# Which gate products run beside the attention heads, and which in their tail: an encoder layer in fp32 on one core

## The chip, the core and the metric

The kernel runs on one core of a Trainium2 chip. Its engines work side by side, each through its own list of instructions in order: TensorE (PE in the profile) multiplies, VectorE (DVE) and ScalarE (ACT) work on elements, GpSimd (POOL) works on elements in SBUF, SyncE (SP) issues most transfers, and ScalarE issues some. SBUF is the working memory, PSUM receives the products in banks, DRAM holds inputs, outputs and spilled intermediate results. The metric is the device time of one execution in microseconds, as the median of several runs; shorter is better.

## The reference

One layer of an encoder, on x of 1024 tokens by 1024 channels in float32:

```
h = rmsnorm(x, g_mix)
z = h @ w_in                      # 512 pooling channels | q | k | v
y_pool = pool_mixer(u_pool)       # windows 2, 4, 8, 16; mean - self; a 128x128 map per group; scale
y_attn = diff_attention(q, k, v)  # 8 heads, two softmax maps each, ALiBi, causal by chunks of 64
gates = sigmoid(h @ w_gate + b_gate)          # 1024 x 2048
merged = gates[:, :1024] * (y_pool @ w_branch_pool) + gates[:, 1024:] * (y_attn @ w_branch_attn)
x = x + merged @ w_out
x = x + square(relu(rmsnorm(x, g_ffn) @ w_up)) @ w_down
```

The change concerns the time in which `gates` (before the sigmoid) and `y_pool @ w_branch_pool` are computed.

## The kernel before, in words

**Products.** Every product of two matrices is made of three matmuls (`mm3`, lines 122 to 124): each operand is split into a high part, rounded to the type that TensorE takes, and a low part, the rest; high times high, high times low and low times high are summed in PSUM. `split` (lines 116 and 117) makes the parts: a cast on ScalarE, then a subtraction on VectorE, or on GpSimd for most weights.

**Heads.** h is normalised and transposed into h^T, which stays in SBUF as parts of high and low for both halves of the tokens. Then eight heads of eight token blocks each go through a pipeline of stages: A makes z (24 matmuls of 384 columns), B normalises q and k, C transposes them, D makes scores and the softmax, E transposes the result, F multiplies by v, H and R norm. The order in a step is written in `O`. The result of a head goes to DRAM (`y_dram`).

**Filler.** The code after the heads traces work that doesn't depend on them, and a scheduler that works through a model of the machine sets it between the heads' instructions: an instruction that comes earlier in the program has the higher priority, and a tile is had when its room (one of a pool's fixed number of buffers) is free. So the list of each engine is fixed at build time. The fillers are

- `pool_group(g)`, the pooling mixer of one of four groups: 48 matmuls, sums on VectorE, then a small product; to `p_dram`.
- `gate_cols(c)`, 128 gate columns computed plainly: two loads of weights, two splits (ScalarE, GpSimd), and for each half of the tokens 24 matmuls of 512 columns and a copy to `g_dram`.
- `gate_first(d)`, the first part of a Strassen scheme for the 2 x 2 blocks of gate columns d and 8 + d: loads A11 and A12, splits both, multiplies the upper left block of h^T (12 matmuls, copied out as x1, then 12 more in the same bank, copied out as C11), then on GpSimd forms S4 = A11 + A12 − A21 − A22 (line 773 adds, line 777 subtracts, twice), splits it, and multiplies (12 matmuls, z3).

Columns 0, 1, 2 and 8, 9, 10 are made plainly (`G_PLAIN = 3`), d = 3 to 7 by the Strassen scheme. `early` is the list of fillers whose steps alternate with those of the pooling groups; the first `G_FIRST` steps stand ahead of them. `late` are the steps whose matmuls are issued behind `z_last[7, 5]`, a late z product of the last head. Before, all six `gate_cols` are early and all five `gate_first` late.

Rooms: raw weights of the filler have two ("fr"), split ones four ("fw"), output copies two ("fo"). In PSUM the filler has one bank (`fill_bank`); `spare_bank` goes round this bank and the two of the heads' z. `gate_first` uses `spare_bank` for d >= `G_Z`. The heads' tiles, the pooling branch's operand (`ypT`) and others share eleven rooms (`ut`); `vt` has six, opened after the fillers. Head weights and the pooling projection's share eight (`wt`) and two raw rooms (`raw`).

**Behind the heads.** The scheme goes on with sums of blocks of h^T, made in place: for each of two parts `kp` eight additions and subtractions of 128 x 1024 (tiles comba, combb, combc, combe, all four "fw" rooms) and four splits back into the rooms of h^T. The pooling branch's projection (`bp`, lines 929 to 936) makes 128 output columns at a time, each of 24 matmuls, copies them into `m` and stores them in `mp_dram`. Then `gate_rest(d)` makes the remaining Strassen products (gA, gB) from the new h^T, the attention output is scaled and split (`load_yT`), and its projection (`ba`) and the merge, the output projection and the MLP follow.

Of the kernel before, what the change touches and what calls it, by code (L numbers as in the profile page):

```python
# [8 lines left out]
F32 = mybir.dt.float32  # L9
# [8 lines left out]
P = 128  # L18
S = 1024
D = 1024  # L20
NT = S // P
NK = D // P
# [23 lines left out]

O = "B1 C2 H6 D3 R7 E4 F5 W-2 A0"
ORDER = [(w[0], int(w[1:])) for w in O.split()]
G_FIRST, G_Z, G_PLAIN = 6, 3, 3

N_OP, N_E1, N_E2, N_R1, N_R2 = 8, 11, 6, 4, 3

# [2 lines left out]
def encoder_kernel(  # L55
# [24 lines left out]
    w_branch_pool, w_branch_attn = w_branch_pool[0], w_branch_attn[0]  # L80
# [24 lines left out]
    def ut(shape, dt, name):  # L105
        return up.tile(shape, dt, tag="U", name=name)

    def raw(shape, name):
        return rpool.tile(shape, F32, tag="raw", name=name)

    def f(ap):
        return ap.bitcast(F32)

    def split(hi, lo, src, lo_eng=None):

        nc.scalar.copy(hi, src)  # L116
        return (lo_eng or nc.vector).tensor_tensor(lo, src, f(hi), op=ALU.subtract)  # L117

    def mm3(ps, lhs_hi, lhs_lo, rhs_hi, rhs_lo, first, last, more=False):

        kw = {"skip_group_check": True} if more else {}
        nc.tensor.matmul(ps, lhs_hi, rhs_hi, start=first, stop=False, **kw)  # L122
        nc.tensor.matmul(ps, lhs_hi, rhs_lo, start=False, stop=False, **kw)  # L123
        return nc.tensor.matmul(ps, lhs_lo, rhs_hi, start=False, stop=last, **kw)  # L124

    def wt(shape, name, dt=F32R):
        return wpool.tile(shape, dt, tag="W", name=name, bufs=N_W)

    def fw_tile(shape, name, dt=F32R):
        return wpool.tile(shape, dt, tag="fw", name=name, bufs=N_FW)  # L130
# [21 lines left out]
    def load_cols2(src, c0, name):  # L152

        rw = raw([P, 4, 2 * P], f"r{name}")
        nc.sync.dma_start(rw, src[0 : 4 * P, c0 : c0 + 2 * P].rearrange("(kk p) c -> p kk c", p=P))
        ws = []
        for j in range(2):
            w = wt([P, 2, 4, P], f"w{name}_{j}")
            split(w[:, 0], w[:, 1], rw[:, :, j * P : (j + 1) * P], nc.gpsimd)
            ws.append([w])  # L160
        return ws
# [12 lines left out]
    def proj_T(ps, ws, rhs, th, nk=NK):  # L174

        for k in range(nk):
            w = ws[k // 4]
            r_hi, r_lo = rhs(k, th)
            mm3(ps, w[:, 0, k % 4, :], w[:, 1, k % 4, :], r_hi, r_lo, k == 0, k == nk - 1)
        return ps  # L180

    def load_split(src, r0, name, tile_fn, scale=None):

        rw = raw([P, S], f"r{name}") if scale is None else wt([P, S], f"r{name}", F32)
        nc.sync.dma_start(rw, src[r0 : r0 + P, :])
        if scale is not None:
            rbs, row = scale
            n = S // len(rbs)
            for i, rb in enumerate(rbs):
                js = slice(i * n, (i + 1) * n)  # L190
                nc.sync.dma_start(rb, row[js].partition_broadcast(P))
                nc.vector.scalar_tensor_tensor(rw[:, js], rw[:, js], gs, rb, op0=ALU.mult, op1=ALU.mult)
        ts = []
        for th in range(2):
            t = tile_fn([P, 2, 512], F32R, f"{name}_{th}", th)
            split(t[:, 0, :], t[:, 1, :], rw[:, th * 512 : (th + 1) * 512])
            ts.append(t)
        return ts
# [6 lines left out]
    def pair(t):  # L205
        return t[:, 0, :], t[:, 1, :]
# [449 lines left out]
    def fill_w(src, c0, name):  # L656
        ws = []
        for j in range(2):
            rw = fr_tile([P, 4, P], f"fr{name}_{j}")
            nc.sync.dma_start(  # L660
                rw, src[j * 512 : (j + 1) * 512, c0 : c0 + P].rearrange("(kk p) c -> p kk c", p=P)
            )
            w = fw_tile([P, 2, 4, P], f"fw{name}_{j}")
            split(w[:, 0], w[:, 1], rw, nc.gpsimd)
            ws.append(w)
        return ws
# [12 lines left out]
    def fill_proj(ws, th, name, bank_fn=fill_bank):  # L679
        ps = bank_fn(name)  # L680
        for k in range(NK):
            w = ws[k // 4]
            mm3(
                ps, w[:, 0, k % 4, :], w[:, 1, k % 4, :],
                hT[k // 2, th, 0][:, k % 2, :], hT[k // 2, th, 1][:, k % 2, :], k == 0, k == NK - 1,
            )
        return ps
# [41 lines left out]
    def gate_cols(c):  # L729
        ws = fill_w(w_gate, c * P, f"gate{c}")  # L730
        for th in range(2):
            ps = fill_proj(ws, th, f"g{c}_{th}")
            keep(ps, g_dram[c * P : (c + 1) * P, th * 512 : (th + 1) * 512], f"go{c}_{th}")
            yield

# [25 lines left out]
    def keep(ps, dst, name):  # L761
        fo = fo_tile(name)[:, 0:512]
        nc.scalar.copy(fo, ps)
        nc.scalar.dma_start(dst, fo)
# [18 lines left out]
        yield  # L783


    early = [gen for d in range(G_PLAIN) for c in (d, NK + d) for gen in [gate_cols(c)] for _ in range(2)]
    late = [gen for gen in map(gate_first, range(G_PLAIN, NK)) for _ in range(2)]
    for _ in range(G_FIRST):
        next(early.pop(0))
    for g in range(4):  # L790
# [2 lines left out]
                next(early.pop(0))  # L793
    for gen in early:
        next(gen)

    vpool = attn.enter_context(tc.tile_pool(name="vpool", bufs=N_V))
    pb = mix.enter_context(tc.tile_pool(name="pb", bufs=5, space=PSUM))
# [2 lines left out]
    def vt(shape, dt, name):  # L801
        return vpool.tile(shape, dt, tag="V", name=name)

    def bank(name):
        nbank[0] += 1
        i = nbank[0] % 8
        if 1 <= i <= 3:
            return (ps_f if i == 3 else ps_z).tile([P, 512], F32, tag="f" if i == 3 else "z", name=name)
        return pb.tile([P, 512], F32, tag="b", name=name)
# [14 lines left out]
    def add(eng, out_, a, b):  # L824
        return eng.tensor_tensor(out_, a, b, op=ALU.add)

    def sub(eng, out_, a, b):
        return eng.tensor_tensor(out_, a, b, op=ALU.subtract)

    dve, pool = nc.vector, nc.gpsimd  # L830


    mp_dram = dram.tile([D, S], F32, name="mp_dram")
    ws_bp = {0: load_cols2(w_branch_pool, 0, "bp0")}
    ypT = [load_split(p_dram, g * P, f"ypT{g}", ypt_tile) for g in range(4)]
    with tc.issue_after(z_last[H - 1, NT - 3].ins):
        for gen in late:
# [3 lines left out]
    for kp in range(2):  # L841
        a, b, c, e = (fw_tile([P, 2, 512], f"comb{n}{kp}", F32) for n in "abce")
        B11, B12, B21, B22 = (
            [hT[kp + 2 * r, th, hl] for hl in range(2)] for r, th in ((0, 0), (0, 1), (1, 0), (1, 1))
        )
        add(dve, a, f(B12[0]), f(B12[1]))
        add(pool, b, f(B22[0]), f(B22[1]))
        add(pool, e, f(B21[0]), f(B21[1]))
        sub(dve, c, b, a)
        sub(dve, a, a, f(B11[0]))  # L850
        sub(dve, a, a, f(B11[1]))
        sub(dve, b, b, a)
        sub(pool, e, e, b)
        for room, t in ((B11, b), (B12, a), (B22, c), (B21, e)):
            split(*room, t)

# [70 lines left out]

    gens = [gate_rest(d) for d in range(G_PLAIN, NK)]
    for d in range(NK):
        if d % 2 == 0 and d + 2 < NK:  # L930
            ws_bp[d + 2] = load_cols2(w_branch_pool, (d + 2) * P, f"bp{d + 2}")
        m = vt([P, S], F32, f"m{d}")
        for th in range(2):
            ps = proj_T(bank(f"bp{d}_{th}"), ws_bp[d - d % 2][d % 2], lambda k, th: pair(ypT[k][th]), th, nk=4)
            nc.scalar.copy(m[:, th * 512 : (th + 1) * 512], ps)
        nc.scalar.dma_start(mp_dram[d * P : (d + 1) * P, :], m)

        if d in (3, 5):
            next(gens[d // 2 - 1])
# [20 lines left out]
    for d in range(NK):  # L960
        if d + 2 < NK:
            ws_ba[d + 2] = load_cols(w_branch_attn, (d + 2) * P, f"ba{d + 2}")
        ws = ws_ba.pop(d)
# [6 lines left out]
        for th in range(2):  # L970
            hs = slice(th * 512, (th + 1) * 512)
            ps = proj_T(bank(f"ba{d}_{th}"), ws, lambda k, th: pair(yT[k][th]), th)
# [60 lines left out]
    def w_out_half(dh, tag, rooms):  # L1033

        ws = {}
        for d in (4, 6, 0, 2) if tag else (0, 2, 4, 6):
            ws[d], ws[d + 1] = load_rows(w_out, d * P, dh * 512, f"o{tag}{dh}_{d}", rooms[d // 4])
        return ws
# [42 lines left out]
    ws = {0: w_out_half(0, 0, (w_room, fw_tile))}  # L1081
    for t in range(4):
        out_proj(ws[0], t, 0)
    ws = {1: w_out_half(1, 1, (w_room, w_room)), 0: w_out_half(0, 1, (h_room, fw_tile))}
# [269 lines left out]
    def operands(j, q):  # L1354
        nraw[0] += 1
        ur = purs[nraw[0] > 2 and nraw[0] % 2].tile([P, 2, 512], F32, tag="ur", name=f"ur{j}_{q}")
        nc.sync.dma_start(ur, ud[SIDES[j][0], q])
        out_ = []
        for n, src, pool_ in (("u", ur, puo), ("w", second(j, q), pwo)):
            hi, lo = (pool_.tile([P, 2, 512], F32R, tag="op", name=f"{n}{j}_{q}{x}") for x in "hl")  # L1360
            split(hi, lo, src, dve)
            out_ += [hi, lo]
        return out_
# [49 lines left out]
    early = {q: operands("1", q) for q in range(3)}  # L1413
# [51 lines left out]
```

## Time and profile before

| | us |
|---|---|
| median of 3 runs (1581.24 to 1581.48) | 1581.39 |
| the profiled execution, its own time | 1580.71 |
| its span, from the first to the last instruction | 1578.9 |
| TensorE busy | 1538.5 |
| VectorE busy | 996.4 |
| ScalarE busy | 825.0 |
| GpSimd busy | 420.8 |

Busy time is the time in which an engine ran at least one instruction; matmuls overlap, so their durations do not add up to it. In a group's row a line number is that of the code, and a tile's name ends where its number began: gA, gB are the banks of the Strassen products, x, C, z their copies, A, S their weights, ga and gr raw gate weights, hT the transposed h, comb its combinations, wbp, ypT, bp and m belong to the pooling projection. A wait's row gives the waiting engine and instruction, then what released it, the total in us, how often and the longest. The granted clock of TensorE is a share of full speed.

### The profile page before, as it was taken

The numbers are of one execution on the slowest core, as the hardware profiler recorded it, in microseconds if no ns is written. First come the engines' busy times: TensorE is split into PE (matmuls) and PEld (weight loads), VectorE is DVE, ScalarE is ACT, GpSimd is POOL, SyncE is SP. The second block draws the span as 40 slices with busy tenths as digits, with TensorE's granted clock in tenths as the row PEclk, the third lists the DMA queues.
The fourth block names the chain that finished last, engine by engine and source line by source line (L and its number), as shares of the span: only waits on it lengthen the run. The fifth ranks groups of instructions, "written<-read, shape, count | busy, mean of one in ns | idle before, by whom it ended". The sixth has DMA issues, their size and how long they took to land.

```text
span 1578.9 us, 21978 instructions
## 1 busy us (share of the span) xinstructions
PE 1538.5 (97%) x7653; PEld 1320.2 (84%) x7653; DVE 996.4 (63%) x1980; ACT 825.0 (52%) x1828; POOL 420.8 (27%) x490
## 2 busy tenths in 40 slices
PE   7999999999999999889999999999999999999999
PEld 6999999999999888667788887788888788888887
DVE  6665767676776776189543358776576568645662
ACT  6656566656566567254443447565555544333331
POOL 5424243434254444664555400000000000000000
PEclk9999999999999999999999999999999999999999
DMA  7112021202021214448865743645443689637750
GB/s 225 61 33 75 21 62 44 62 19 85 14 63 51 64 62 145 155 147 282 260 232 166 233 145 103 198 136 165 153 160 114 244 302 360 219 126 241 225 193 27
DMA packets 177545, 223.98 MB, mean 142 GB/s; under 512 B 10565, under 2 KB 111130, under 8 KB 177434
## 3 DMA queue, kind: packets, MB, share of 16 engines
q1 hardware_dynamic: 159594, 192.39, 37.6%
q10 hardware_dynamic: 17840, 30.19, 5.1%
q8 instruction: 60, 0.98, 0.3%
q14 instruction: 51, 0.42, 0.1%
HBM read 161.16 MB, written 61.37 MB: 141 GB/s over the span
## 4 chain that ended last, share of the span: by engine, by line
PE 81%; DVE 6%; DMA 6%; ACT 3%; POOL 2%; issue 1%; SPq 1%; ACTq 0%; POOLq 0%; DVEq 0%
PE z L122 5%; PE z L123 5%; PE z L124 5%; PE Da L123 4%; PE Da L122 4%; PE Da L124 4%; PE Db L123 3%; PE Db L122 3%; PE Db L124 3%; PE X L124 2%; PE X L122 2%; PE X L123 2%; PE sc L492 2%; PE sc L493 2%; PE op L124 2%; PE op L122 2%
## 5 line engine op out<-in xcount | busy, mean ns | idle before, releaser
L123 PE MATMUL z<-wqkv,hT 128*128 128x384 f32 x512 | 175.7, 344 | 0.7 <-POOL wqkv L117 0.6
L122 PE MATMUL z<-wqkv,hT 128*128 128x384 f32 x512 | 175.4, 343 | 0.3
L124 PE MATMUL z<-wqkv,hT 128*128 128x384 f32 x512 | 173.8, 340 | 0.4 <-DVE hT L117 0.3
L503 ACT ACTIVATE s<-s,nm 128x256 f32<-128x256 f32 (+7 forms) x128 | 99.7, 779 | 46.6 <-DVE nm L495 44.6
L433 POOL TENSOR_TENSOR ms<-ms,mhalf 128x4 f32<-128x4 f32 x64 | 71.6, 1118 | 165.1 <-DVE ms L431 163.1
L122 PEld LDWEIGHTS z<-wqkv,hT 128*128 128x128 f32 x512 | 97.0, 190 | 4.8 <-DVE qn L436 1.7
L123 PEld LDWEIGHTS z<-wqkv,hT 128*128 128x128 f32 x512 | 97.2, 190 | 4.6 <-POOL wqkv L117 1.8
L124 PEld LDWEIGHTS z<-wqkv,hT 128*128 128x128 f32 x512 | 96.9, 189 | 3.3 <-DVE hT L117 1.2
L495 DVE CUSTOM_DVE_ANT_0 s<-sc,dist 128x512 f32<-128x512 f32 (+3 forms) x128 | 74.8, 586 | 22.0 <-PE sc L493 20.0
L492 PE MATMUL sc<-K,Q 128*128 128x512 f32 (+2 forms) x192 | 69.1, 364 | 0.5 <-DVE nm L495 0.3
L493 PE MATMUL sc<-K,Q 128*128 128x512 f32 (+2 forms) x192 | 66.7, 354 | 0.0
L117 DVE TENSOR_TENSOR AS<-s,AS 128x512 fp32r<-128x512 f32 x64 | 43.8, 688 | 35.6 <-ACT AS L116 35.4
L117 POOL TENSOR_TENSOR wqkv<-rqkv,wqkv 128x384 fp32r<-128x384 f32 x60 | 60.9, 1034 | 6.1 <-ACT wqkv L116 6.0
L442 POOL TENSOR_TENSOR qn<-qn,ggh 128x128 f32<-128x128 f32 x64 | 32.8, 513 | 107.7 <-DVE qn L436 98.9
L463 DVE TENSOR_TENSOR K<-tk,K 64x128 fp32r<-64x128 f32 x128 | 37.0, 289 | 24.4 <-ACT K L462 20.4
L123 PE MATMUL ba<-yT,wba 128*128 128x512 f32 x128 | 50.7, 396 | 0.9 <-DVE yT L117 0.9
L464 ACT CAST Q<-tk 64x128 fp32r<-64x128 f32 x128 | 33.0, 258 | 35.4 <-DVE K L463 34.0
L124 PE MATMUL ba<-yT,wba 128*128 128x512 f32 x128 | 50.5, 395 | 0.0
L122 PE MATMUL ba<-yT,wba 128*128 128x512 f32 x128 | 50.5, 396 | 0.0
L122 PE MATMUL op<-wo,mT 128*128 128x512 f32 x128 | 50.2, 396 | 0.0
L123 PE MATMUL op<-wo,mT 128*128 128x512 f32 x128 | 50.2, 394 | 0.0
L466 ACT CAST Q<-tk 64x128 fp32r<-64x128 f32 x128 | 33.2, 259 | 32.4 <-DVE Q L465 29.7
(489 smaller groups left out, 4837.3 us busy)
## 6 DMA issues: line engine op xcount, KB each, us to landing
wd<-in_w_down_dram SPq DMA_DIRECT2D x56, 512.0 KB, 6.1
wu<-in_w_up_dram SPq DMA_DIRECT2D x32, 512.0 KB, 5.2
udS<-us SPq DMA_DIRECT2D x64, 256.0 KB, 3.1
ur<-udS SPq DMA_DIRECT2D x32, 512.0 KB, 3.4
rqkv<-in_w_in_dram SPq DMA_DIRECT2D x64, 192.0 KB, 2.9
ud<-u ACTq DMA_DIRECT2D x48, 256.0 KB, 3.1
ur<-ud SPq DMA_DIRECT2D x24, 512.0 KB, 7.2
ga<-in_w_gate_dram SPq DMA_DIRECT2D x25, 256.0 KB, 2.8
```

Of the source, the lines that this page charges most:

```text
L117: return (lo_eng or nc.vector).tensor_tensor(lo, src, f(hi), op=ALU.subtract)
L122: nc.tensor.matmul(ps, lhs_hi, rhs_hi, start=first, stop=False, **kw)
L123: nc.tensor.matmul(ps, lhs_hi, rhs_lo, start=False, stop=False, **kw)
L124: return nc.tensor.matmul(ps, lhs_lo, rhs_hi, start=False, stop=last, **kw)
L433: nc.gpsimd.tensor_tensor(ms, ms, mhalf[:, 0:4], op=ALU.pow)
L463: nc.vector.tensor_tensor(K[other, m, c0 : c0 + P], k, f(k_hi), op=ALU.subtract)
L464: nc.scalar.copy(q_hi, q)
L466: nc.scalar.copy(Q[other, m, 1, :], q)
L492: nc.tensor.matmul(dst, Q[:, i, 0, :], rhs, start=True, stop=False)
L493: nc.tensor.matmul(dst, Q[:, i, 1, :], rhs, start=False, stop=True)
L495: nc.vector.tensor_tensor_reduce(out=s[i][:, c : c + w], in0=sc[:, 0:w], in1=dist[:, o0 + c : o0 + c + w], scale=2.0 ** -(h + 1), scalar=B ...
L503: nc.scalar.activation(s[i][:, 0:n], s[i][:, 0:n], AF.Exp, bias=last, scale=-1.0, accum_out=Z[:, i, t : t + 1])
```

## The change

- `G_FIRST` goes from 6 to 4, `G_Z` from 3 to 7. The first four plain steps (columns 0 and 8) stay early; behind them, alternating with the pooling groups, come the ten steps of `gate_first`. The remaining eight plain steps (columns 1, 9, 2, 10) become the late ones.
- Those late plain products use `spare_bank`; of the Strassen ones only `gate_first(7)` still does.
- The additions B22, B21 and the last subtraction of each round of combinations go from GpSimd to VectorE, and the sum of B21 is made at the end.
- The pooling projection's weights are all loaded ahead of `ypT`, where before the first pair was, and the others in the loop; `m` takes a room of `ut` in place of one of `vt`.

```diff
-G_FIRST, G_Z, G_PLAIN = 6, 3, 3
+G_FIRST, G_Z, G_PLAIN = 4, 7, 3
...
     def gate_cols(c):
         ws = fill_w(w_gate, c * P, f"gate{c}")
         for th in range(2):
-            ps = fill_proj(ws, th, f"g{c}_{th}")
+            ps = fill_proj(ws, th, f"g{c}_{th}", spare_bank if c % NK else fill_bank)
...
-    early = [gen for d in range(G_PLAIN) for c in (d, NK + d) for gen in [gate_cols(c)] for _ in range(2)]
-    late = [gen for gen in map(gate_first, range(G_PLAIN, NK)) for _ in range(2)]
+    plain = [gen for d in range(G_PLAIN) for c in (d, NK + d) for gen in [gate_cols(c)] for _ in range(2)]
+    early, late = plain[:G_FIRST], plain[G_FIRST:]
+    early += [gen for gen in map(gate_first, range(G_PLAIN, NK)) for _ in range(2)]
     for _ in range(G_FIRST):
         next(early.pop(0))
...
-    ws_bp = {0: load_cols2(w_branch_pool, 0, "bp0")}
+    ws_bp = {d: load_cols2(w_branch_pool, d * P, f"bp{d}") for d in range(0, NK, 2)}
...
         add(dve, a, f(B12[0]), f(B12[1]))
-        add(pool, b, f(B22[0]), f(B22[1]))
-        add(pool, e, f(B21[0]), f(B21[1]))
+        add(dve, b, f(B22[0]), f(B22[1]))
         sub(dve, c, b, a)
         sub(dve, a, a, f(B11[0]))
         sub(dve, a, a, f(B11[1]))
         sub(dve, b, b, a)
-        sub(pool, e, e, b)
+        add(dve, e, f(B21[0]), f(B21[1]))
+        sub(dve, e, e, b)
...
     for d in range(NK):
-        if d % 2 == 0 and d + 2 < NK:
-            ws_bp[d + 2] = load_cols2(w_branch_pool, (d + 2) * P, f"bp{d + 2}")
-        m = vt([P, S], F32, f"m{d}")
+        m = ut([P, S], F32, f"m{d}")
```

## The prediction

> **What bounds the kernel now.** The page says that TensorE is busy for nearly the whole span, so a reordering that leaves its products alone can win only the time in which it stands still or is clocked down.
>
> ```profile
> span 1578.9 us, 21978 instructions
> PE 1538.5 (97%) x7653; PEld 1320.2 (84%) x7653; DVE 996.4 (63%) x1980; ACT 825.0 (52%) x1828; POOL 420.8 (27%) x490
> ```
>
> 40.4 us are idle. The table by stretches shows where around the change: the columns are the stretch, its length, the busy time of each engine with its instructions, TensorE's granted clock and the DMA share.
>
> ```profile
> 40.00:560.00 520.00, 517.65 (x3081) 481.74 (x3080) 351.89 (x1062) 324.00 (x970) 205.78 (x289) 1.00 0.16 50
> ...
> 582.70:640.00 57.30, 52.63 (x283) 44.17 (x282) 35.98 (x95) 38.54 (x96) 26.92 (x27) 0.99 0.44 140
> 640.00:660.00 20.00, 16.70 (x62) 12.60 (x61) 1.23 (x1) 4.52 (x9) 13.13 (x11) 0.86 0.62 191
> ...
> 660.00:701.30 41.30, 41.30 (x179) 33.32 (x178) 25.38 (x16) 16.81 (x27) 27.44 (x14) 1.00 0.39 135
> 701.30:718.30 17.00, 9.06 (x26) 6.41 (x26) 16.97 (x12) 7.68 (x12) 12.89 (x6) 0.70 0.60 198
> 718.30:767.60 49.30, 45.54 (x197) 36.30 (x196) 43.08 (x55) 22.84 (x41) 21.43 (x13) 1.00 0.83 271
> 708.60:718.20 9.60, 7.61 (x19) 5.59 (x20) 9.60 (x9) 5.01 (x9) 5.59 (x3) 0.56 0.87 286
> 639.00:642.10 3.10, 3.08 (x7) 2.50 (x8) 0.51 (x3) 1.37 (x4) 1.62 (x2) 0.51 0.99 277
> 648.60:652.30 3.70, 3.28 (x8) 2.09 (x9) 0.00 (x0) 0.28 (x2) 3.57 (x3) 0.54 0.96 306
> ...
> L124 PE MATMUL z<-wqkv,hT x512: 331/336/687, 12.7 to 582.7; 128*128 128x384 f32 x171
> ```
>
> Under the heads (40 to 560) TensorE loses 2.35 us of 520. In the heads' tail, from the last z product (last row, 582.7) to 660, it loses 4.67 + 3.30 = **8.0 us**; where h^T is recombined (701.3 to 718.3) 17.00 − 9.06 = **7.9 us**; in the gates behind it 3.8 us. The three rows with clocks of 0.51 to 0.56 are matmuls that ran at about half clock after a wait. Busy time × (1 − clock) is what they lost: 3.08 × 0.49 = 1.5, 3.28 × 0.46 = 1.5 and 7.61 × 0.44 = 3.3 us. All that can be won here is 8.0 + 7.9 + 3.8 + 6.3 = 26.0 us. The row 660 to 701.3 also gives the price of a 512-column matmul: 41.30 / 179 = 0.231 us.
>
> TensorE's waits name the causes, first 582.7 to 701.3, then 701.3 to 767.6.
>
> ```profile
> PE gA L122 <- ACT x L763: 4.3, 2, 3.0
> PE gB L122 <- ACT S L116: 2.9, 1, 2.9
> PE bp L122 <- ACT rT L602: 0.3, 1, 0.3
> PE po L123 <- DVE AT_0l L117: 0.3, 1, 0.3
> ...
> PE gA L122 <- ACT hT L116: 6.0, 1, 6.0
> PE gA L123 <- DVE hT L117: 1.9, 1, 1.9
> PE gA L124 <- DVE S L117: 1.7, 1, 1.7
> ```
>
> In the tail 7.2 us are waits of the Strassen products (gA, gB) on their own preparation. GpSimd shows why.
>
> ```profile
> L777 POOL TENSOR_TENSOR ga<-ga,ga 128x512 f32<-128x512 f32 x8 | 10.3, 1290 | 23.5 <-DMA ga<-in_w_gate_dram 20.8 <-DVE nm L495 2.8
> ...
> 589.75 1.29 POOL L773 TENSOR_TENSOR ga<-ga,ga 128x512 f32<-128x512 f32 x1
> 608.64 1.30 POOL L773 TENSOR_TENSOR ga<-ga,ga 128x512 f32<-128x512 f32 x1
> 626.36 1.26 POOL L773 TENSOR_TENSOR ga<-ga,ga 128x512 f32<-128x512 f32 x1
> 650.98 1.27 POOL L773 TENSOR_TENSOR ga<-ga,ga 128x512 f32<-128x512 f32 x1
> ```
>
> L773 stands once in each gate_first(d): the distances are 18.9, 17.7 and 24.6 us. With two raw rooms ("fr"), A11 and A12 are loaded and split, added, then A21 loaded and subtracted, then A22. Each such chain feeds 36 matmuls, 8.3 us of TensorE. So the tail's filler takes its pace from a chain of loads.
>
> **The stall at 701** starts earlier, on VectorE. The fence holds rows of the timelines of VectorE, TensorE and GpSimd, then two stretches with the projection's matmuls alone.
>
> ```profile
> 643.08 1.23 DVE L825 TENSOR_TENSOR comba<-hT,hT 128x1024 f32<-128x1024 f32 x1 [3.37 <-PE gB L124]
> 675.72 1.23 DVE L828 TENSOR_TENSOR combc<-combb,comba 128x1024 f32<-128x1024 f32 x1 [31.41 <-PE gB L124]
> ...
> 675.23 0.39 PE L124 MATMUL gB<-hT,S 128*128 128x512 f32 x1
> ...
> 708.65 0.80 PE L122 MATMUL gA<-hT,S 128*128 128x512 f32 x1 [6.00 <-ACT hT L116]
> ...
> 707.44 2.28 DVE L117 TENSOR_TENSOR hT<-comba,hT 128x1024 fp32r<-128x1024 f32 x1
> ...
> 681.81 3.32 POOL L828 TENSOR_TENSOR combe<-combe,combb 128x1024 f32<-128x1024 f32 x1 [11.04 <-DVE combb L828]
> ...
> 650.00:675.60 25.60, 20.72 (x83) 0.96 0.34 113
> 675.60:701.40 25.80, 25.68 (x110) 1.00 0.45 153
> ```
>
> The combinations take all four "fw" rooms and overwrite h^T, so they wait until the last first product has left, 675.6. The gates' products need both rounds of them and go on at 708.65: **33 us** of combinations. The pooling projection (last two rows) had 83 of its matmuls drawn forward into the chain's gaps, so only 110 × 0.231 = 25 us were left as cover, and 33 − 25 = 8 us is the stall.
>
> **The change, part by part.** Products are only exchanged. Under the heads now run five gate_first (180 matmuls) in place of four gate_cols (192). Held for the tail are four gate_cols, 192 × 0.231 = 44.4 us against 41.6. gate_first(7) is written as early, but draws on the z banks, which the heads' z products claim first; I expect it at the tail's start, where it is more filler and ends the heads' z products as much earlier. The sum of matmuls is unchanged.
>
> *Tail.* A held-back gate_cols needs two loads and two splits:
>
> ```profile
> L116 ACT CAST fwgate<-frgate x12: 620/622/684, 26.5 to 370.7; 128x512 fp32r<-128x512 f32 x12
> L117 POOL TENSOR_TENSOR fwgate<-frgate,fwgate x12: 1276/1290/1626, 27.2 to 371.7; 128x512 fp32r<-128x512 f32 x12
> L763 ACT COPY go<-g x12: 564/587/608, 43.7 to 486.5; 128x512 f32<-128x512 f32 x12
> ...
> ga<-in_w_gate_dram SPq DMA_DIRECT2D x25, 256.0 KB, 2.8
> mp_dram<-m ACTq DMA_DIRECT2D x8, 512.0 KB, 3.0
> ```
>
> Load, cast and split are 2.8 + 0.6 + 1.3 = 4.7 us for a half, some 6 for both, beneath 48 matmuls of 11.1 us; four rooms hold two columns' weights, three banks let the copy-out (0.6) pass. So the chain is shorter than its products and the 7.2 us of waits go, with the 3.0 us of half clock behind them. What could come back: nothing, or one chain of 6 us less what the heads' own products cover (0 to 3 us). I take 1.5. The projection's weights, now loaded at once, add no instruction, but three loads and six splits (6 × 1.3 = 7.8 us) move ahead of ypT's loads on SP and of the tail's splits on GpSimd. The heads' products cover them; uncovered, they make the first held-back column up to 7.8 us late, which the first rival prices.
>
> *Combinations.* Three adds of each of two rounds go to VectorE. The row at 643.08 gives 1.23 us alone, that at 707.44 2.28 beside GpSimd: 7.4 to 13.7 us more on VectorE, less the waits on GpSimd (the 3.3 us row). What matters is the cover. With 8.0 + 3.0 − 1.5 us saved ahead of it, all products and the projection end at about 701.3 − 9.5 = 691.8; if the held-back products go first, the last leaves 192 × 0.231 = 44.4 us before, at 647. Then 33 us of combinations end at 680, and with 13.7 more at 694. So the 7.9 us stall and 3.3 us of half clock go, and from 0 (680) to 694 − 691.8 = 2.2 us return; I take 1.0, since less GpSimd work stands beside.
>
> The Trainium skill, "SBUF — State Buffer", section "Who interferes with whom", says that a VectorE instruction with two SBUF inputs and a GpSimd instruction that reads SBUF exclude each other for the whole instruction. By that rule the trace agrees: 1.23 us against 2.28. The sum of this part stays as it is, but the rule speaks against the early side of the change, and the third rival takes that up.
>
> *Under the heads.* One gate_first issues four loads, three stores, three casts, three copies, three splits and three adds on GpSimd; one gate_cols two of each but the adds. The exchange is +30 − 8 = 22 GpSimd operations × 1.29 = 28.4 us, seven casts and seven copies more on ScalarE (7 × (0.62 + 0.59) = 8.5 us), twelve loads more on SP. GpSimd is busy 206 of 520 us there and ScalarE 324, so both have room; TensorE covers it, because z products stand ready while a filler waits. On GpSimd the heads' powers and weight splits are queued behind a subtraction that waits for its load (20.8 us in eight such waits above, 2.6 each). Uncovered, five chains × 2 subtractions × 2.6 = 26 us; with two steps between z and the transposes I take a cost of 2, bounds 0 and 10.
>
> *Projection's rooms.* m takes a room of the attention's pool: no operation more. ypT fills eight of eleven, three stay for m, whose 24 matmuls last 5.5 us and whose store lands in 3.0 us. The matmuls of the other two rooms hide copy and store, so nothing; without them one store, 3.0 us.
>
> *The gates behind* (3.8 us): the splits that they wait for stand behind scaling work in VectorE's order, which the change leaves. I count no gain, bound 3.8.
>
> **Sum:** −7.2 − 3.0 + 1.5 − 7.9 − 3.3 + 1.0 + 2.0 = −16.9 us. The profiled execution is 1580.7 us (1578.9 of span and 1.8 around); this gives 1563.8. The median of the runs is 0.7 above the profiled one: **1564.5**. With every gain and no cost it is 1581.4 − 26.0 = 1555.4.
>
> The Trainium skill, "TensorE: Matmul & The Clock Gate", section "What's actually happening", puts the fall to half clock after an idle window of about 3.4 us. By that rule the trace does not quite agree: it has half clock after waits of 2.9 and 3.0. By the Trainium skill the 3.0 us in the tail would not be counted, and the sum would be 1567.5.
>
> **The rivals.**
>
> *Only the tail gains* (0.15). If the held-back products leave late, at about 667 (33 us before 700, 8 us behind the projection's end at 692), the projection fills in between as before, and the stall stays. For: it did so before (83 of its matmuls). Against: the plain chain is shorter than its products. 1581.4 − 7.2 − 3.0 + 1.5 + 2.0 = 1574.7.
>
> *The cover is spent first: slower* (0.12). The projection now has all weights early and rooms of its own, so it can be drawn into the tail ahead of the last held-back product. The stall is then 33 us less what is left of it. Won in the tail are about 10.2 us, and the old loss was 11.2; so it decides from a stall of 21.4 − 3.3 = 18 us, that is with less than 15 us, 65 of its 192 matmuls, left. With 40 left: 33 − 9.2 + 3.3 = 27.1, against 21.4: 1587. Against it: ypT waits for rooms of the heads.
>
> ```profile
> L116 ACT CAST ypT<-rypT x8: 616/622/641, 622.0 to 634.4; 128x512 fp32r<-128x512 f32 x8
> ```
>
> It was ready at 635 only, 12 us before 647: at most 52 matmuls could go ahead.
>
> *The heads pay* (0.08). If each of the 30 early GpSimd operations holds one VectorE instruction for 2.28 − 1.23 = 1.05 us, VectorE, busy 352 of 520 us there, loses 31 us. Were half to reach TensorE, in place of the 2.0: 1564.5 − 2.0 + 15.5 = 1578; the exchange would have moved the idle time from the tail into the heads and done nothing. For: a GpSimd neighbour did cost an addition 1.05. Against: VectorE's instructions there with two large inputs in SBUF are few.
>
> ```profile
> L512 DVE SCALAR_TENSOR_TENSOR s<-s,cf,s 128x640 f32<-128x640 f32 (+3 forms) x28 | 31.2, 1115 | 0.5
> L512 DVE SCALAR_TENSOR_TENSOR s<-s,cf 128x128 f32<-128x128 f32 (+3 forms) x28 | 16.1, 575 | 0.6
> ```
>
> They are 47 of the 352 us. The section of the Trainium skill named above ("SBUF — State Buffer", "Who interferes with whom") makes the blocking certain wherever the two meet; how often they meet, only the result shows.
>
> **Chances.** The forecast 0.65, with its own range 1556 to 1571. A measurement here tells 0.2%, 3.2 us, from no change. Faster: 0.65 + 0.15, less a little of each, and half of the last: 0.79. Same: 0.09, from the last rival and mild forms of the second. Slower: 0.12. The range 1555 to 1580 takes in both bounds of the costs; it leaves out the slower rival and a part of the last above, 0.16, and 0.04 below.
>
> **What would show it.** Right: 582 to 700 without waits on x or S; the chain of L773 standing between 100 and 560; the combinations starting near 647 and ending before the projection's last matmul; full clock from 640 to 720; the same work from 800 on, only earlier. Wrong: waits of z, sc or tk on GpSimd between 100 and 560; the stall on hT still there, with fewer of the projection's matmuls behind the last held-back product.

## The result, and the profile after

The changed kernel takes **1565.14 us** (median of 4 runs, 1562.48 to 1566.65) against 1581.43 (4 runs, 1581.24 to 1582.65) for the kernel before on the same chip: a ratio of 0.9894, with a 95% interval of 0.9876 to 0.9911. That is 16.3 us less; 1564.5 was forecast. The profiled execution is the slowest of the four, 1566.65 us with a span of 1564.8, so what follows explains 14.1 us of span.

The page of the kernel after, first its span and then each engine's busy time with its share and its instructions:

```profile
span 1564.8 us, 21964 instructions
PE 1534.5 (98%) x7653; PEld 1319.8 (84%) x7653; DVE 992.4 (63%) x1986; ACT 824.6 (53%) x1828; POOL 401.5 (26%) x484
```

TensorE's idle time has gone from 40.4 to 30.3 us, and its busy time is 4.0 us shorter although it has the same 7653 matmuls: fewer of them ran at half clock. 10.1 + 4.0 = 14.1.

The table by stretches of the kernel after (stretch, length, busy time of the engines with their instructions, granted clock, DMA share, GB/s):

```profile
40.00:560.00 520.00, 515.96 (x3088) 481.38 (x3088) 362.59 (x1086) 332.64 (x996) 230.46 (x313) 1.00 0.19 59
573.40:640.00 66.60, 66.58 (x345) 56.11 (x344) 38.23 (x93) 38.48 (x93) 20.70 (x25) 1.00 0.38 121
640.00:660.00 20.00, 18.12 (x86) 14.69 (x85) 16.85 (x17) 7.87 (x14) 12.40 (x6) 1.00 0.31 100
660.00:697.30 37.30, 33.00 (x131) 26.04 (x130) 17.92 (x19) 14.20 (x23) 7.74 (x6) 0.91 0.65 225
...
718.00:767.00 49.00, 45.60 (x199) 36.69 (x198) 35.44 (x42) 21.54 (x35) 26.10 (x15) 1.00 0.77 250
```

The groups of the z products, of the plain gate products, of the projection's and of the Strassen chain's addition, each with its least, median and longest ns and then its first and last start:

```profile
L124 PE MATMUL z<-wqkv,hT x512: 331/335/686, 12.3 to 573.4; 128*128 128x384 f32 x171
L124 PE MATMUL g<-hT,fwgate x96: 387/390/478, 31.8 to 642.2; 128*128 128x512 f32 x96
L122 PE MATMUL bp<-ypT,wbp x64: 390/394/795, 642.4 to 696.6; 128*128 128x512 f32 x64
L773 POOL TENSOR_TENSOR ga<-ga,ga x5: 1290/1294/1300, 122.0 to 453.7; 128x512 f32<-128x512 f32 x5
```

The tail of the heads, from 573.4 to 640, has no idle time left (0.02 us), and the Strassen chain (last row) stands under the heads. All of the projection (bp) now follows the last plain product (g, 642.2). But from 640 to 697.3 a new hole has opened: 1.9 + 4.3 us idle, and 33.00 × (1 − 0.91) = 3.0 us of half clock. TensorE's waits from 560 to 790 name it:

```profile
PE trr L600 <- POOL r L598: 4.0, 1, 4.0
PE gA L122 <- ACT uv L893: 2.3, 1, 2.3
PE bp L122 <- ACT m L935: 1.9, 1, 1.9
PE ba L123 <- DVE yT L117: 1.1, 1, 1.1
PE bp L122 <- ACT rT L602: 0.3, 1, 0.3
```

None of the old waits on x, S or h^T is among them. The new ones are the transpose of r, the last head's norm factor (trr), and the projection's output room m. The timelines of VectorE, GpSimd, ScalarE and TensorE show how they come about (start, duration, engine, line, operation; in brackets the idle time before it and what ended it; merged instructions have their number behind the x):

```profile
650.48 1.27 DVE L594 TENSOR_TENSOR r<-SS,rz 128x8 f32<-128x8 f32 x1
...
658.37 1.09 DVE L117 TENSOR_TENSOR S<-ga,S 128x512 fp32r<-128x512 f32 x1 [3.15 <-ACT S L116]
659.38 2.31 DVE L830 TENSOR_TENSOR combc<-combb,comba 128x1024 f32<-128x1024 f32 x1
661.61 1.21 DVE L827 TENSOR_TENSOR combe<-hT,hT 128x1024 f32<-128x1024 f32 x1
662.75 0.16 DVE L596 TENSOR_SCALAR r<-r 128x8 f32<-128x8 f32 x1
...
647.45 4.28 POOL L827 TENSOR_TENSOR s<-gr 128x512 f32<-128x512 f32 x1 [31.71 <-DMA gr<-in_w_gate_dram]
651.81 3.38 POOL L830 TENSOR_TENSOR gr<-ga,gr 128x512 f32<-128x512 f32 x1
656.39 1.29 POOL L830 TENSOR_TENSOR ga<-s,ga 128x512 f32<-128x512 f32 x1
662.98 2.55 POOL L597 TENSOR_TENSOR r<-r,mhalf 128x8 f32<-128x8 f32 x1 [2.38 <-DVE r L596]
...
657.72 0.62 ACT L116 CAST S<-ga 128x512 fp32r<-128x512 f32 x1 [6.60 <-POOL ga L830]
658.24 0.58 ACT L935 COPY m<-bp 128x512 f32<-128x512 f32 x1
...
665.89 0.37 PE L600 MATMUL trr<-identf,r 128*8 128x128 f32 x1 [3.96 <-POOL r L598]
674.22 1.23 DVE L117 TENSOR_TENSOR hT<-combe,hT 128x1024 fp32r<-128x1024 f32 x1 [0.25 <-ACT hT L116]
```

Read it from the middle. GpSimd forms the gates' weight sums (s, gr, ga); its first two take 4.28 and 3.38 us, while VectorE runs the combinations back to back, where the same operation takes 1.29 a moment later. ScalarE waits 6.6 us for such a sum to cast it, and a copy of the projection's output (m) stands behind this cast: the 1.9 us wait. VectorE's split S waits for that cast, and behind it in VectorE's list stand two operations of the combinations and then L596, the third step of the norm, a matter of 0.16 us. So the power on GpSimd starts at 662.98, and TensorE, which comes to the transpose at 661.9, stands before it until 665.89. The combinations themselves are done by 674.22 + 1.23 = 675.5, 22 us before the projection is.

### The profile page after: what moved, and what is told of

Same layout as the page of the kernel before. It is cut to its first block, busy times and chain, and to the rows that moved or that the text cites. A ratio compares the mean times of both kernels' runs of the same rounds, so it can differ in the third digit from the quotient of the medians.

```text
span 1564.8 us, 21964 instructions
## 1 busy us (share of the span) xinstructions
PE 1534.5 (98%) x7653; PEld 1319.8 (84%) x7653; DVE 992.4 (63%) x1986; ACT 824.6 (53%) x1828; POOL 401.5 (26%) x484
## 4 chain that ended last, share of the span: by engine, by line
PE 85%; DVE 5%; DMA 4%; ACT 2%; issue 1%; POOL 1%; SPq 1%; ACTq 0%; DVEq 0%; POOLq 0%
PE z L122 5%; PE z L123 5%; PE z L124 5%; PE Da L123 4%; PE Da L122 4%; PE Da L124 4%; PE Db L123 3%; PE Db L122 3%; PE Db L124 3%; PE X L124 3%; PE X L122 3%; PE X L123 2%; PE sc L492 2%; PE sc L493 2%; PE op L124 2%; PE op L122 2%
## 5 line engine op out<-in xcount | busy, mean ns | idle before, releaser
L465 DVE TENSOR_TENSOR Q<-tk,Q 64x128 fp32r<-64x128 f32 x128 | 36.6, 286 | 22.7 <-ACT Q L464 20.9
L122 PE MATMUL op<-wo,mT 128*128 128x512 f32 x128 | 50.2, 396 | 0.0
L466 ACT CAST Q<-tk 64x128 fp32r<-64x128 f32 x128 | 33.2, 260 | 32.3 <-DVE Q L465 30.1
L123 PE MATMUL op<-wo,mT 128*128 128x512 f32 x128 | 50.2, 394 | 0.0
L124 PE MATMUL op<-wo,mT 128*128 128x512 f32 x128 | 50.1, 393 | 0.0
```

Of the source, the lines that this page charges most:

```text
L465: nc.vector.tensor_tensor(Q[own, m, 1, :], q, f(q_hi), op=ALU.subtract)
L466: nc.scalar.copy(Q[other, m, 1, :], q)
```

## The experiments

The first question is which part of the change does the work. **Only the fillers are exchanged:**

```diff
-G_FIRST, G_Z, G_PLAIN = 6, 3, 3
+G_FIRST, G_Z, G_PLAIN = 4, 7, 3
...
-            ps = fill_proj(ws, th, f"g{c}_{th}")
+            ps = fill_proj(ws, th, f"g{c}_{th}", spare_bank if c % NK else fill_bank)
...
-    early = [gen for d in range(G_PLAIN) for c in (d, NK + d) for gen in [gate_cols(c)] for _ in range(2)]
-    late = [gen for gen in map(gate_first, range(G_PLAIN, NK)) for _ in range(2)]
+    plain = [gen for d in range(G_PLAIN) for c in (d, NK + d) for gen in [gate_cols(c)] for _ in range(2)]
+    early, late = plain[:G_FIRST], plain[G_FIRST:]
+    early += [gen for gen in map(gate_first, range(G_PLAIN, NK)) for _ in range(2)]
```

> The fillers are exchanged as in the change; combinations stay on GpSimd and the pooling projection's rooms stay. Theory (the order of the fillers brings the gain: the tail's chain waits, 10 us with the clock, and by an earlier last product the cover of the combinations, 11 us): 1563 to 1568, the stall on hT gone though the combinations still take some 33 us. Rival (the faster combinations bring the second half): about 1575, with the waits of gA on hT still there, 6 to 8 us.

Measured: 1567.86 us, a ratio of 0.9917 (0.9896 to 0.9938). TensorE's two longest waits from 560 to 790:

```profile
PE trr L600 <- POOL r L598: 10.3, 1, 10.3
PE gA L124 <- DVE S L117: 1.2, 1, 1.2
```

The exchange takes away the waits of the tail and the stall on h^T, and gives 13.7 us (1581.56 − 1567.86), which is not told apart from the whole change (the intervals overlap). It leaves one long wait, 10.3 us for the same r; a third of 0.7 us is all that stands beside these two.

**Only the combinations are moved to VectorE:**

```diff
-        add(pool, b, f(B22[0]), f(B22[1]))
-        add(pool, e, f(B21[0]), f(B21[1]))
+        add(dve, b, f(B22[0]), f(B22[1]))
...
-        sub(pool, e, e, b)
+        add(dve, e, f(B21[0]), f(B21[1]))
+        sub(dve, e, e, b)
```

> Only the combinations go to VectorE, in the kernel of before. Theory: they start at 675 as before, so the stall is at most shortened by the waits on GpSimd, 0 to 5 us: 1576 to 1583, waits in the tail unchanged at some 7 us. Rival (they bring half of the gain): 1573 or below, no wait on hT.

Measured: 1577.23 us, 0.9973 (0.9957 to 0.9989). The two longest waits from 560 to 790:

```profile
PE gA L122 <- ACT x L763: 3.4, 1, 3.4
PE gB L122 <- ACT S L116: 3.4, 1, 3.4
```

The waits on x and S stay, as they must, and no wait on h^T is left: with all additions on VectorE that stall goes by itself, also with the old order. So the missing wait is the rival's, but the time is the theory's: of the 11.2 us that the stall and its half clock came to, 4.3 are won. Behind it the gates' products now wait for their weights (2.5 us on S is the longest of these waits), and from 720 to 770 TensorE runs at 0.93, where it ran at 1.00 before.

**Only the projection's rooms and its early weights:**

```diff
-    ws_bp = {0: load_cols2(w_branch_pool, 0, "bp0")}
+    ws_bp = {d: load_cols2(w_branch_pool, d * P, f"bp{d}") for d in range(0, NK, 2)}
...
-        if d % 2 == 0 and d + 2 < NK:
-            ws_bp[d + 2] = load_cols2(w_branch_pool, (d + 2) * P, f"bp{d + 2}")
-        m = vt([P, S], F32, f"m{d}")
+        m = ut([P, S], F32, f"m{d}")
```

> Only the pooling projection's weights are loaded at once and m takes a room of ut, in the kernel of before. Theory: no gain of its own, 1579 to 1584. Rival (the cover is spent first): the projection is drawn further into the tail, more than 83 of its 192 matmuls before the last first product, the stall on hT grows, 1585 to 1592.

Measured: 1588.73 us, 1.0049 (1.0034 to 1.0064): **slower**. TensorE's two longest waits from 560 to 790:

```profile
PE gA L122 <- ACT hT L116: 7.0, 1, 7.0
PE sc L492 <- DVE nm L495: 3.3, 1, 3.3
```

The stretch from 580 to 600 of its table:

```profile
580.00:600.00 20.00, 16.70 (x72) 13.34 (x71) 10.41 (x29) 11.73 (x34) 15.95 (x18) 0.83 0.43 138
```

And of GpSimd's timeline, four splits of the projection's weights:

```profile
578.95 5.44 POOL L117 TENSOR_TENSOR wbp<-rbp,wbp 128x512 fp32r<-128x512 f32 x4 [0.45 <-ACT wbp L116]
```

Ahead of the last first product stood 86 of the projection's matmuls, against 83 before, 0.7 us of cover; of the waits on h^T one grew by 1.0 us and the other shrank by 1.5. So the time is that of the slower rival, but its path doesn't explain it. Four weight splits hold GpSimd for 5.44 us from 579 on, among the heads' last steps, and four more follow by 593; before, only two of them stood there. In this stretch TensorE lost 3.3 us and ran at 0.83, where before it was busy for all 20.00 us at 1.00. Other losses came in behind the heads: the gates wait 3.1 us for a weight's low part S, where it was 1.7. That the splits cause the waits is read from their place; neither they nor the room of m was tried apart.

**The change without its rooms, and the change without its combinations.** Beside the changed kernel, the first takes back the rooms' lines shown above, the second the combinations'.

> The whole change but the pooling projection's weights and rooms. Theory: like the change, 1562 to 1568. Rival (the projection's weights come too late without it and TensorE waits on wbp or the cover is cut): 1570 or more, with waits of bp on wbp.

> The change with the combinations left on GpSimd as before. Theory: with the last product at 642 and 33 us of combinations they are still covered: 1561 to 1569, so VectorE's share in the gain is small. Rival (without VectorE the combinations outlast the projection): 1570 or more, waits of gA on hT.

Measured: 1568.19 us without the rooms, 0.9920 (0.9903 to 0.9937), and 1569.63 without the combinations, 0.9924 (0.9901 to 0.9948). The longest wait, first without the rooms:

```profile
PE trr L600 <- POOL r L598: 12.1, 1, 12.1
```

then without the combinations:

```profile
PE trr L600 <- POOL r L598: 10.4, 1, 10.4
```

With the exchange, either part alone leaves r's wait at 10 to 12 us; only both together bring it to the 4.0 of the whole change. By their times these two, the exchange alone and the whole change can't be told apart. The loss that the rooms make in the old order doesn't show here.

**Does the chain of loads set the tail's pace?** In the kernel before, S4 is made without loading A21 and A22; A11 is subtracted in their place, so the gates are not the reference's:

```diff
         for q in (21, 22):
-            nc.gpsimd.tensor_tensor(r12, r12, gate_raw(q, d), op=ALU.subtract)
+            nc.gpsimd.tensor_tensor(r12, r12, r11, op=ALU.subtract)
```

> The kernel of before, but S4 is made without the loads of A21 and A22: A11, which is in its room already, is subtracted twice in their place (left out: two loads of each first product). Theory (the tail's filler takes its pace from the chain of loads): the distances of L773 fall from about 19 us to below 12, the tail's waits on x and S (7.2 us) and their half clock (3 us) mostly go, and as the last product leaves earlier, the combinations too: 1566 to 1574. Rival (the pace is set by the bank, the copies or the heads' latency): distances and time as before, 1579 to 1582.

Measured: 1581.82 us, 1.0002 (0.9986 to 1.0017). Rows of GpSimd's timeline, the first two being the first and the last of the four additions L773 of the tail:

```profile
586.66 1.30 POOL L773 TENSOR_TENSOR ga<-ga,ga 128x512 f32<-128x512 f32 x1
...
624.65 1.30 POOL L773 TENSOR_TENSOR ga<-ga,ga 128x512 f32<-128x512 f32 x1
...
660.37 3.31 POOL L828 TENSOR_TENSOR combe<-combe,combb 128x1024 f32<-128x1024 f32 x1
663.65 1.64 POOL L597 TENSOR_TENSOR r<-r,mhalf 128x8 f32<-128x8 f32 x1
672.68 1.19 POOL L598 TENSOR_TENSOR r<-r,rz 128x8 f32<-128x8 f32 x1
```

And TensorE's longest wait:

```profile
PE trr L600 <- POOL r L598: 19.2, 1, 19.2
```

The distances fall from 18.9, 17.7 and 24.6 us to (624.65 − 586.66) / 3 = 12.7 on average (below 12 was expected), and the waits on x and S go, but for 0.3 us: the chain did set the pace. Yet the time is the rival's and nothing is won, since the norm of the last head takes over. Its last step on VectorE is done at 653.6; its two steps on GpSimd stand behind weight splits and combinations, and TensorE waits 19.2 us for them.

**The short chain with that norm left out** (the transpose takes 1/Z in place of r in the last head):

```diff
-            nc.vector.tensor_tensor(r, SS[h], rz, op=ALU.mult)
...
+            if h < H - 1:
+                nc.vector.tensor_tensor(r, SS[h], rz, op=ALU.mult)
...
-            nc.tensor.transpose(tr[0:NT, 0:P], r, identf)
+            nc.tensor.transpose(tr[0:NT, 0:P], rz if h == H - 1 else r, identf)
```

> The kernel of before with the short chain of e6_short_chain (A11 subtracted in place of loading A21 and A22) and without the last head's norm: the transpose takes 1/Z, which is there early (left out besides those loads: five small operations of one head). Theory (the tail's gain of the short chain was only hidden behind the wait for that norm, 19 us in the run before): that wait goes and the time falls to 1564 to 1573. Rival (the short chain gains nothing, and the wait for the norm only stood where the stall on hT would have been): 1578 to 1583, with a wait on hT or S of 8 us or more in its place.

Measured: 1575.32 us, 0.9953 (0.9938 to 0.9969). The two longest waits left:

```profile
PE ta L549 <- DVE s L512: 3.9, 1, 3.9
PE gA L122 <- ACT uv L892: 3.8, 1, 3.8
```

The time lies between the theory's and the rival's. A shorter chain is worth some 7 us once the norm doesn't stand behind it. That is less than was set free: the waits on x and S are gone, with their half clock 10.2 us in the kernel before, and the stall on h^T is gone too, 11.2 with its own. Much of it comes back as other waits, of which the longest are shown.

**What do the combinations still cost?** They are left out altogether, in the kernel before and in the changed one, so the gates' later products are of an h^T that is not combined:

```diff
-    for kp in range(2):
-        a, b, c, e = (fw_tile([P, 2, 512], f"comb{n}{kp}", F32) for n in "abce")
...
-        for room, t in ((B11, b), (B12, a), (B22, c), (B21, e)):
-            split(*room, t)
```

> The kernel of before without the combinations: h^T is left as it is for the gates' second products (left out: 16 additions of 128 x 1024 and 8 splits). Theory: what the combinations cost there is the stall and its half clock, 11 us: 1568 to 1572. Rival (their cost is spread, through VectorE's and GpSimd's time in the gates behind): 1560 to 1566.

> The changed kernel without the combinations (left out as in the run before it). Theory: they are covered by the pooling projection's 55 us; what goes with them is only the 6 us of waits at 657 to 667 (m behind a cast, the norm's transpose behind the combinations) and 3 us of half clock: 1555 to 1560. Rival (these waits don't come from the combinations): 1563 to 1566.

Measured: 1569.4 us for before without them, 0.9931 (0.9905 to 0.9957), and **1554.99** for the changed kernel without them, 0.9833 (0.9811 to 0.9856). Before, they cost 12 us, where the stall and its half clock came to 11.2. In the changed kernel they still cost 10 us, although they end 22 us before they are needed. The only wait left from 560 to 790 in the changed kernel without them:

```profile
PE gA L122 <- ACT uv L878: 2.2, 1, 2.2
```

**The norm ahead.** Theory: those 10 us are not the combinations' own lateness but that of the norm queued behind them. So in the changed kernel the second round of the combinations is issued behind the norm's last step on VectorE, and the gates' weight sums behind its last step on GpSimd; all work is done:

```diff
-            nc.vector.tensor_scalar(r, r, 1.0 / P, EPS, op0=ALU.mult, op1=ALU.add)
+            norm_last[0] = nc.vector.tensor_scalar(r, r, 1.0 / P, EPS, op0=ALU.mult, op1=ALU.add)
...
-            nc.gpsimd.tensor_tensor(r, r, rz, op=ALU.mult)
+            norm_last[1] = nc.gpsimd.tensor_tensor(r, r, rz, op=ALU.mult)
...
+        if kp:
+            late_norm.enter_context(tc.issue_after(norm_last[0].ins))
...
-        add(pool, s1, r21, r22)
...
+        with tc.issue_after(norm_last[1].ins):
+            add(pool, s1, r21, r22)
...
```

> The changed kernel with the last head's norm ahead: the second round of combinations on VectorE and the sums of the gates' weights on GpSimd are issued behind it. Theory (the 6 us of waits and 3 us of half clock at 657 to 667 come from the norm's place in these two lists): no wait of trr over 1 us, 1555 to 1561. Rival (the norm is late by its own chain, or the wait passes on to the gates' first products): 1562 to 1568.

Measured: **1556.08 us** (1555.01 to 1558.23), 0.9835 (0.9816 to 0.9853), which beats both kernels; the interval doesn't touch that of the change. The only wait from 560 to 790:

```profile
PE gA L122 <- ACT uv L900: 2.9, 2, 2.7
```

The two stretches in which the changed kernel had its hole:

```profile
640.00:660.00 20.00, 20.00 (x92) 16.24 (x91) 19.61 (x20) 7.66 (x13) 9.42 (x5) 1.00 0.32 100
660.00:697.30 37.30, 37.30 (x163) 30.40 (x162) 21.09 (x25) 18.56 (x32) 14.09 (x9) 1.00 0.85 293
```

And from the timelines the end of the norm on VectorE and on GpSimd:

```profile
650.25 0.17 DVE L598 TENSOR_SCALAR r<-r 128x8 f32<-128x8 f32 x1
650.50 2.55 POOL L599 TENSOR_TENSOR r<-r,mhalf 128x8 f32<-128x8 f32 x1 [35.67 <-DVE r L598]
653.13 0.89 POOL L600 TENSOR_TENSOR r<-r,rz 128x8 f32<-128x8 f32 x1
```

r is ready at 654.0, before TensorE comes to the transpose at 657.6; in the changed kernel the transpose had to wait until 665.9. From 640 to 697 TensorE doesn't idle for a moment. The 9.1 us won (1565.14 − 1556.08; 9.3 by the two ratios) are what the hole was worth: 1.9 + 4.3 idle and 3.0 of half clock, 9.2. With the combinations done the kernel is as fast, to 1.1 us, as without them. So what they still cost in the changed kernel was a matter of order: that of the norm's five operations of 128 x 8 among them and the weight sums, and that of the copy of m behind the cast of such a sum (the 1.9 us). Both lists were changed at once, so what each is worth was not tried apart.

**The same, with the first gate's sums on VectorE** in place of GpSimd:

```diff
+        eng = dve if d == G_PLAIN else pool
         with tc.issue_after(norm_last[1].ins):
-            add(pool, s1, r21, r22)
+            add(eng, s1, r21, r22)
...
```

> As e14_norm_ahead, and the first of the gates' weight sums (three of 128 x 512) on VectorE. Theory (what is left is GpSimd and VectorE blocking each other: these sums took 3.4 and 4.3 us beside the combinations in place of 1.3): 0 to 2 us better than e14_norm_ahead. Rival (VectorE is the bound there): 1 to 3 us worse.

Measured: 1562.87 us, 0.9876 (0.9855 to 0.9897), about 7 us worse than with the sums on GpSimd, where the rival had 1 to 3. The run doesn't tell the load from the place: in VectorE's list the three sums stand ahead of and between the norm's steps (the last of them right ahead of L598, the third step), not behind them. No profile of an execution near this time was kept, so where the time went stays open.

**The exchange and the norm ahead, without the other two parts.** The edits of the first experiment and of the norm, in the kernel before, its combinations on GpSimd and VectorE as they were (the second round's on GpSimd are issued behind the norm's last step there).

> The kernel before, with the fillers exchanged as in the change, the combinations left on GpSimd and VectorE as before, the rooms as before, and the second round of the combinations and the gates' weight sums issued behind the last head's norm. Theory (the exchange frees the tail, and all that the other two parts of the change add is a shorter wait for the last head's norm): with the norm ahead, the transposes wait at most 2 us for r, and the time is 1555 to 1561 us. Rival (the combinations have to be on VectorE as well): GpSimd still stands between the norm's steps with weight splits and the first round, the transposes wait 4 us or more for r, and the time is 1563 to 1568 us.

Measured: 1567.42 us (1563.44 to 1568.53), 0.9898 (0.9866 to 0.9929). The longest wait from 560 to 790:

```profile
PE trr L602 <- POOL r L600: 4.6, 1, 4.6
```

And rows of the timelines of VectorE and GpSimd:

```profile
650.80 1.23 DVE L598 TENSOR_SCALAR r<-r 128x8 f32<-128x8 f32 x1
643.87 8.14 POOL L117 TENSOR_TENSOR wbp<-rbp,wbp 128x512 fp32r<-128x512 f32 x4 [1.87 <-ACT wbp L116]
652.12 2.55 POOL L599 TENSOR_TENSOR r<-r,mhalf 128x8 f32<-128x8 f32 x1
```

The theory fell, and the time and the wait are the rival's: four weight splits occupy GpSimd for 8.14 us until the moment at which the power can begin, and the norm's last step on VectorE, 0.17 us in the norm-ahead run, takes 1.23 and ends at the same time. With the norm ahead as well, the other two parts of the change are worth some 10 us (0.9898 − 0.9835 = 0.63%), and the two intervals don't touch. The wait of 4.6 us and the half clock behind it (6.60 × 0.44 = 2.9 from 655.5 to 662.5) are most of that. Which of the two parts is needed for it, this run doesn't tell: GpSimd's splits end at 652.0, and VectorE's step too. Nor is r alone to blame. It is ready at 655.5, only 1.5 us later than with the norm ahead in the changed kernel, but TensorE comes to the transpose at 651.0, not at 657.6: the place that the scheduler gives the transpose counts as well, and it was not varied by itself.

## Why the prediction was right, and where it was not

The forecast of 1564.5 us holds to 0.6 us, but its sum was less exact than that. Against the profiled execution it had −16.9 us, and the two spans differ by 14.1. So part of the hit is luck: a term too small by 8 us was made up in large part by gains that the sum had not counted, and the execution profiled after lies 1.5 us above its median, where the forecast had set the median 0.7 above the profiled one.

- **The tail** (−7.2 − 3.0 + 1.5). Right, and better than forecast: from 573.4 to 640 nothing is idle (8.0 us before up to 660) and the clock is 1.00, so the 1.5 us taken for new chains did not come. As foreseen, the last Strassen first product stands at the tail's start, and the heads' z products end 9.3 us earlier. The reason given, a chain of loads that sets the pace, is shown by the short chain's distances. The step that didn't hold is that its price was owed to it alone: with the chain shortened in the old order, the norm's wait takes all of it.
- **h^T's recombination** (−7.9 − 3.3 + 1.0). The stall and its half clock are gone, and the combinations end at 675.5 rather than at 680 to 694. They end early because they begin early, not because they are faster: their first subtraction (combc) runs at 637.05, ahead of the last held-back product (642.2), where the forecast let them wait for that product until 647. From this subtraction to their last split they take 38.4 us, against 37.3 before (675.72 to 709.65 + 3.38). But the term that was to return was **mis-sized: 1.0 forecast, 9.2 measured** (1.9 + 4.3 idle, 3.0 of half clock). The step that failed: the sum asked only when the combinations would be ready for their own readers, the gates' products. It should have asked what else stands among them in VectorE's and GpSimd's lists. That was the last head's norm, whose transpose stands in TensorE's list in the midst of the projection (and, for 1.9 us of the 9.2, the copy of m behind a cast in ScalarE's list). "Full clock from 640 to 720" was wrong for the same reason (0.91 from 660 to 697).
- **Under the heads** (+2.0). 1.7 us measured (520 − 515.96 against 520 − 517.65). GpSimd took 24.7 us more (28.4 forecast), ScalarE 8.6 (8.5), and TensorE covered it. The size holds, but not the path, and that is luck: no wait there on GpSimd is over 0.4 us, and the longest, 1.3 us, is a Strassen product behind a copy on ScalarE (u, of the pooling mixer).
- **The rooms** (nothing). In the whole change this can't be told from what was measured, by its time. As a statement on that edit it is wrong: alone, in the old order, it costs 0.49%. If the splits are the cause, the heads' products did not cover them there, the case that the prediction priced at up to 7.8 us: 7.2 were measured, though through several waits and not through the first held-back column.
- **The gates behind** (no gain). 3.4 us idle after, 3.8 before: right.
- **What makes up the difference.** Gone: 8.0 + 3.0 + 7.9 + 3.3 + 0.4 = 22.6 us; back: 9.2 + 1.7 = 10.9; net 11.7. A further 1.7 us went at the heads' end. The row of before, with all its idle time ahead of the last z product:

```profile
560.00:582.70 22.70, 20.99 (x136) 20.06 (x135) 17.39 (x56) 14.74 (x48) 10.66 (x15) 1.00 0.20 65
```

After, TensorE is busy for all of 560 to 573.4. The remaining 0.7 us is shorter busy time of TensorE elsewhere, which was not traced: 14.1 in all. The prediction did not count the heads' end among what can be won.

The rivals: "only the tail gains" falls, as no wait on h^T is left. "The cover is spent first" falls, as all of the projection follows the last held-back product (642.4 against 642.2); the rooms alone did lose time, but in another way. "The heads pay" falls with the 1.7 us.

The prediction weighed two rules. The Trainium skill, "SBUF — State Buffer", section "Who interferes with whom", lets a VectorE instruction with two SBUF inputs and a reading GpSimd instruction exclude each other. The trace after agrees, but GpSimd alone loses: its sums take 4.28 and 3.38 us where one takes 1.29, beside VectorE's additions that keep their 1.21. Before, at 707.44, both were stretched: VectorE's split to 2.28 us and GpSimd's sum beside it (706.40) to 2.25. And the addition at 643.08, which the prediction read as "alone", stood beside this row:

```profile
643.32 3.36 POOL L117 TENSOR_TENSOR wbp<-rbp,wbp 128x512 fp32r<-128x512 f32 x2
```

Its 1.23 us is right all the same (GpSimd is idle beside the 1.23 at 675.72), but the two splits took 3.36 us, where the next two took 2.50: GpSimd was the loser there already. The prediction looked for this cost beneath the heads; it was paid here, behind them. The Trainium skill, "TensorE: Matmul & The Clock Gate", section "What's actually happening", has half clock after an idle window of about 3.4 us. The waits after agree with it: the granted clock was 1.00 behind those of 1.9 us (656 to 660) and 2.3 us (735 to 740), and 0.50 behind that of 4.0 (665.9 to 671). The half clock after 2.9 and 3.0 us in the kernel before still does not, nor does a clock of 0.53 (724.4 to 727.6) behind a wait of 2.2 us in the changed kernel without the combinations. So in these runs the length of a wait alone doesn't settle it.

## What to carry to other kernels

When work is moved to another engine, look not only for its readers but for every small instruction that comes after it in that engine's list, and ask which of them releases the bottleneck: here the place of five operations of 128 x 8, and of a copy behind one cast, decided some 9 us. A wait that is removed uncovers the next one, so a shortened chain without a gain doesn't prove that it was not the limit: remove the next wait too before you judge. Nor do the parts of a change add up, so try them together as well as alone: one of these cost 7 us by itself and did no harm that could be measured beside the others.

## What was not expected of the hardware

- A small operation can take several times as long beside a large one of the other engine: the norm's steps on 128 x 8 took 1.27 us on VectorE beside GpSimd's sums in the changed kernel, and 0.16 and 0.17 with the norm ahead, where GpSimd was idle. The power on GpSimd took 1.64 or 2.55 us. Which operation holds the other back at each place was not tried apart.
- On GpSimd, an addition of 128 x 512 took 1.29 us alone and up to 4.28 beside back-to-back additions on VectorE, a factor of 3.3; in the kernel before VectorE's operations stretched as well, from 1.23 to 2.28 us.
